# An interleaved rotary embedding: the first megabyte of x in two DMAs of 64 partitions on two queues

## The chip, the cores and the metric

The kernel runs on one core of one Trainium2 chip. The metric is the device time of the program in microseconds, the median of several executions. A profile is one execution more, recorded by the hardware profiler. The engines named below are DVE (VectorE), ACT (ScalarE), POOL (GpSimd) and SP (SyncE); SP and ACT can issue DMAs on hardware queues, POOL issues them on the software queue. All of them are carried out by the core's 16 DMA engines.

## The reference

`x` has the shape (8, 2048, 16, 64): batch, position, head, element, in float32. `cos` and `sin` have the shape (2048, 32). Each pair of neighbouring elements is rotated by the angle of its position:

```python
x_pairs = x.reshape(batch, seq_len, num_heads, head_dim // 2, 2)
x1 = x_pairs[..., 0]
x2 = x_pairs[..., 1]
out1 = x1 * cos - x2 * sin
out2 = x1 * sin + x2 * cos
out = np.stack([out1, out2], axis=-1)
```

The result has the shape of `x` and is float32 again. `x` is 64 MiB and the result is 64 MiB; the tables are 0.25 MiB each.

## The kernel before, in words

The 2048 positions of a batch lie over 128 partitions, 16 neighbouring positions (`K`) in each. A position's 16 heads of 64 elements make a row of 1024 elements, so a batch is a tile of 128 partitions by 16 rows, `xt`, which the kernel keeps in bf16 (4 MiB). There are five such tiles (`NX`), used in turn for the eight batches.

Loads and stores of whole tiles go through POOL's software queue, which converts between float32 in memory and bf16 in the tile (`load`, line 56; `store`, line 59). DVE does the arithmetic in `rotate`: a product with the sine table into `qt` (line 74), a product with the cosine table in place (line 75), and the sum of the two with the neighbours of each pair exchanged (line 80). The sine table holds plus and minus sin alternately, the cosine table each cos twice, both in bf16.

The order of the work is written out by hand (`manual_schedule`); each engine carries out its own list in order.

At the start, SP issues three plain DMAs: the first two rows (`HEAD`) of batch 0 in float32 into a staging tile (`head`, shown as `st`), 8 KiB for each partition and 1 MiB in all (line 84), then `cos` and `sin` (lines 85 and 86). POOL issues five casting loads without waiting: the other 14 rows of batch 0, and batches 1 to 4. ACT converts the staged megabyte to bf16 into the first rows of batch 0's tile (line 91). DVE waits for `sin` and `cos`, makes the tables (lines 93 to 97), and then rotates the first two rows of batch 0, the other 14, and batches 1 to 7.

After each batch POOL issues its store, and from batch 1 on the load of batch b + 4 into the tile that batch b - 1 has left, which waits for that store. After batch 1, POOL first copies one element of the fifth tile (`mark`, line 106), which holds it until that load has landed. Of the last batch 12 rows go out through POOL. The last 4 rows (`TAIL`) are converted to float32 by ACT (line 118) and issued by SP (line 119); ahead of it, a copy of one element on ACT (line 117) waits for the store of the batch before.

The staging tiles and `qt` share one buffer (`tag="work"`), so the first product of DVE also waits for ACT's conversion of the staged megabyte.

Of the kernel before, what the change touches and what calls it, by code (L numbers as in the profile page):

```python
# [2 lines left out]

# [4 lines left out]


@with_exitstack  # L10
def kernel(
    ctx: ExitStack,
    tc: tile.TileContext,
    x: bass.AP,
    cos: bass.AP,
    sin: bass.AP,
    out: bass.AP,
):
    nc = tc.nc
    fp32 = mybir.dt.float32  # L20
    bf16 = mybir.dt.bfloat16
    mult = mybir.AluOpType.mult
    add = mybir.AluOpType.add

    B, S, H, D = x.shape
    P = 128
    K = S // P
    KP = 16
    D2 = D // 2
    HD = H * D  # L30
    NX = 5
    HEAD = 2
    TAIL = 4


    x_t = x.rearrange("b (p k) h d -> b p k (h d)", p=P, k=K)
    out_t = out.rearrange("b (p k) h d -> b p k (h d)", p=P, k=K)
    cos_t = cos.rearrange("(p k) c -> p (k c)", p=P, k=K)
    sin_t = sin.rearrange("(p k) c -> p (k c)", p=P, k=K)

    consts = ctx.enter_context(tc.tile_pool(name="consts", bufs=1))
    xpool = ctx.enter_context(tc.tile_pool(name="xpool", bufs=NX))
    stage = ctx.enter_context(tc.tile_pool(name="stage", bufs=1))

    cos_sb = consts.tile([P, K * D2], fp32)
    sin_sb = consts.tile([P, K * D2], fp32)
    c_tab = consts.tile([P, K, D], bf16)
    s_tab = consts.tile([P, K, D], bf16)

    mark = consts.tile([1, 1], bf16)  # L50
    tiles = {}

    def load(b, k0=0):
        if b not in tiles:
            tiles[b] = xpool.tile([P, K, HD], bf16, name="xt")
        nc.gpsimd.dma_start(out=tiles[b][:, k0:], in_=x_t[b, :, k0:])  # L56

    def store(b, k1=K):
        nc.gpsimd.dma_start(out=out_t[b, :, :k1], in_=tiles[b][:, :k1])  # L59

    def rotate(b, k0, k1):
        nk = k1 - k0
        xp = tiles[b][:, k0:k1]
        qt = stage.tile([P, KP, HD], bf16, name="qt", tag="work")

        def rows(a):
            return a.rearrange("p k (h e) -> p k h e", h=H, e=D)

        def tab(a):
            return dataclasses.replace(  # L70
                a, offset=a.offset + k0 * D, ap=[a.ap[0], [D, nk], [0, H], [1, D]]
            )

        nc.vector.tensor_tensor(out=rows(qt[:, :nk]), in0=rows(xp), in1=tab(s_tab), op=mult)  # L74
        nc.vector.tensor_tensor(out=rows(xp), in0=rows(xp), in1=tab(c_tab), op=mult)  # L75
        q_swap = dataclasses.replace(
            qt, offset=qt.offset + 1, ap=[qt.ap[0], [2, nk * HD // 2], [-1, 2]]
        )
        x3 = xp.rearrange("p k (a j) -> p (k a) j", j=2)
        nc.vector.tensor_tensor(out=x3, in0=x3, in1=q_swap, op=add)  # L80

    with tc.manual_schedule():
        head = stage.tile([P, TAIL, HD], fp32, name="st", tag="work")
        nc.sync.dma_start(out=head[:, :HEAD], in_=x_t[0, :, :HEAD])
        nc.sync.dma_start(out=cos_sb, in_=cos_t)
        nc.sync.dma_start(out=sin_sb, in_=sin_t)
        load(0, HEAD)
        for b in range(1, NX):
            load(b)

        nc.scalar.copy(out=tiles[0][:, :HEAD], in_=head[:, :HEAD])  # L91
        s2 = s_tab.rearrange("p k (i j) -> p (k i) j", j=2)
        nc.vector.tensor_copy(out=s2[:, :, 0], in_=sin_sb)  # L93
        nc.vector.tensor_scalar_mul(s2[:, :, 1], sin_sb, -1.0)  # L94
        nc.vector.tensor_copy(  # L95
            out=c_tab.rearrange("p k (i j) -> p (k i) j", j=2),
            in_=cos_sb.to_broadcast([P, K * D2, 2]),
        )
        for b in range(B):
            if b == 0:  # L100
                rotate(b, 0, HEAD)
                rotate(b, HEAD, KP)
            else:
                rotate(b, 0, KP)
            if b == 1:
                nc.gpsimd.tensor_copy(out=mark, in_=tiles[NX - 1][:1, K - 1, :1])  # L106
            if b < B - 1:
                store(b)

            if b >= 1 and b - 1 + NX < B:  # L110
                load(b - 1 + NX)
        store(B - 1, K - TAIL)

        tail = stage.tile([P, TAIL, HD], fp32, name="st", tag="work")
        nc.scalar.copy(out=tiles[B - 2][:1, 0, :1], in_=tiles[B - 1][:1, K - 1, :1])  # L117
        nc.scalar.copy(out=tail, in_=tiles[B - 1][:, K - TAIL :])  # L118
        nc.sync.dma_start(out=out_t[B - 1, :, K - TAIL :], in_=tail)


# [1 line left out]
_INS = ['x', 'cos', 'sin']  # L123
_OUTS = [((8, 2048, 16, 64), 'float32')]


# [23 lines left out]
```

## Time and profile before

| | |
|---|---|
| median of 3 runs | 317.52 us (317.23 to 317.98) |
| span of the profiled execution | 315.5 us |
| DVE busy | 210.3 us, 67% |
| ACT busy | 6.9 us, 2% |
| POOL busy | 11.7 us, 4% |
| read from and written to memory | 67.63 MB and 67.11 MB |
| first megabyte of x, issue to landing | 4.7 us |
| cos and sin, issue to landing | 13.4 us and 31.7 us |
| tail of 2 MB on SP, issue to landing | 15.5 us |

The profiled execution's own time is its span, from the first instruction to the last; the runs were timed without a profile, and their median is 2.0 us above it. The slices of the page cut the span into 40 equal parts and give each engine's busy share in tenths. A window's line gives its bounds and length, then for DVE, ACT and POOL the busy time with the number of instructions, the granted clock of TensorE (not used here), the busy share of the DMA engines, and GB/s. In short windows a share can be above 1, since a packet counts as a whole where it stands. A line of the waits names who waited, for what, how long in all, how many times, and the longest wait.

### The profile page before, as it was taken

What the parts mean: (1) busy time and instruction counts of PE and PEld (TensorE: products, weight loads), DVE (VectorE), ACT (ScalarE), POOL (GpSimd) and SP (SyncE); (2) the same over time, 40 slices, a digit from 0 to 9 for tenths busy, and PEclk for the clock granted to TensorE, in tenths of its full rate; (3) what the DMA queues carried; (4) which work ended last, traced back from release to release, by engine and by line L of the source; (5) the groups of instructions that cost most, each with busy time, mean ns of one, the idle gap of its engine ahead of it and who ended that gap; (6) DMA issues with size and microseconds to landing.
All of it is one profiled execution on the core that took longest, in us unless ns stands there. A gap on an engine that the chain in (4) does not pass through costs nothing.

```text
span 315.5 us, 125 instructions
## 1 busy us (share of the span) xinstructions
DVE 210.3 (67%) x30; ACT 6.9 (2%) x4; POOL 11.7 (4%) x21
## 2 busy tenths in 40 slices
DVE  0000799999999999999999993899509994000000
ACT  4000000000000000000000000000000000000400
POOL 3000000000000301010000100000000000000000
DMA  9899999999999999999999999999999999999997
GB/s 279 184 261 206 199 220 245 199 199 253 212 199 266 399 449 482 399 332 245 220 399 399 399 199 199 399 532 266 199 241 490 399 399 490 440 399 399 432 432 332
DMA packets 2880, 101.71 MB, mean 322 GB/s; under 512 B 320, under 2 KB 320, under 8 KB 576
## 3 DMA queue, kind: packets, MB, share of 16 engines
q0 software_dynamic: 2304, 98.04, 97.1%
q1 hardware_dynamic: 576, 3.67, 3.0%
HBM read 67.63 MB, written 67.11 MB: 427 GB/s over the span
## 4 chain that ended last, share of the span: by engine, by line
another core or an unknown queue 91%; DMA 1%; ACTq 1%; ACT 1%; issue 0%
DMA st<-in_x_dram 1%; ACTq L145 1%; ACT xt L91 1%; ACT xt L117 0%; ACTq L117 0%
## 5 line engine op out<-in xcount | busy, mean ns | idle before, releaser
L74 DVE TENSOR_TENSOR qt<-xt,s_tab 128x16384 bf16<-128x16384 bf16 (+2 forms) x9 | 69.7, 7743 | 19.1 <-DMA xt<-in_x_dram 18.8
L75 DVE TENSOR_TENSOR xt<-xt,c_tab 128x16384 bf16<-128x16384 bf16 (+2 forms) x9 | 69.7, 7743 | 0.4
L80 DVE TENSOR_TENSOR xt<-xt,qt 128x16384 bf16<-128x16384 bf16 (+2 forms) x9 | 69.7, 7744 | 0.3
L93 DVE CAST s_tab<-sin_sb 128x512 bf16<-128x512 f32 x1 | 0.5, 453 | 33.4 <-DMA sin_sb<-in_sin_dram 33.4
L59 POOL DMA_DIRECT2D out_dram<-xt x8 | 4.3, 534 | 139.9 <-DVE xt L80 139.9
L56 POOL DMA_DIRECT2D xt<-in_x_dram x8 | 4.4, 560 | 72.8 <-DMA out_dram<-xt 72.0
L117 ACT COPY xt<-xt 1x1 bf16<-1x1 bf16 x1 | 0.2, 192 | 288.0 <-DMA out_dram<-xt 288.0
L106 POOL COPY mark<-xt 1x1 bf16<-1x1 bf16 x1 | 2.9, 2929 | 39.6 <-DMA xt<-in_x_dram 39.6
L118 ACT CAST st<-xt 128x4096 f32<-128x4096 bf16 x1 | 3.6, 3598 | 0.0
L91 ACT CAST xt<-st 128x2048 bf16<-128x2048 f32 x1 | 1.9, 1897 | 3.4 <-DMA st<-in_x_dram 3.4
L91 ACT ACT_TABLE_LOAD x1 | 1.3, 1283 | 0.7 <-PEq L134 0.7
L95 DVE CAST c_tab<-cos_sb 128x1024 bf16<-128x1024 f32 x1 | 0.7, 683 | 0.0
L94 DVE TENSOR_SCALAR s_tab<-sin_sb 128x512 bf16<-128x512 f32 x1 | 0.4, 444 | 0.0
L134 POOL MEMSET const-float32-0.0<- 128x1 f32 x1 | 0.1, 100 | 0.2 <-issue 0.2
L134 POOL MEMSET const-bfloat16-1.0<- 128x1 bf16 x1 | 0.1, 102 | 0.0
L134 POOL MEMSET const-float32-1.0<- 128x1 f32 x1 | 0.1, 100 | 0.0
L134 POOL MEMSET const-uint8-127<- 128x1 uint8 x1 | 0.1, 100 | 0.0
## 6 DMA issues: line engine op xcount, KB each, us to landing
xt<-in_x_dram POOLq DMA_DIRECT2D x7, 4096.0 KB, 57.6
out_dram<-xt POOLq DMA_DIRECT2D x1, 6144.0 KB, 47.8
xt<-in_x_dram POOLq DMA_DIRECT2D x1, 3584.0 KB, 22.3
out_dram<-st SPq DMA_DIRECT2D x1, 2048.0 KB, 15.5
st<-in_x_dram SPq DMA_DIRECT2D x1, 1024.0 KB, 4.7
cos_sb<-in_cos_dram SPq DMA_DIRECT2D x1, 256.0 KB, 13.4
sin_sb<-in_sin_dram SPq DMA_DIRECT2D x1, 256.0 KB, 31.7
out_dram<-xt POOLq DMA_DIRECT2D x7, 70.1
```

The lines of the kernel that those rows point to most:

```text
L56: nc.gpsimd.dma_start(out=tiles[b][:, k0:], in_=x_t[b, :, k0:])
L59: nc.gpsimd.dma_start(out=out_t[b, :, :k1], in_=tiles[b][:, :k1])
L74: nc.vector.tensor_tensor(out=rows(qt[:, :nk]), in0=rows(xp), in1=tab(s_tab), op=mult)
L75: nc.vector.tensor_tensor(out=rows(xp), in0=rows(xp), in1=tab(c_tab), op=mult)
L80: nc.vector.tensor_tensor(out=x3, in0=x3, in1=q_swap, op=add)
L91: nc.scalar.copy(out=tiles[0][:, :HEAD], in_=head[:, :HEAD])
L93: nc.vector.tensor_copy(out=s2[:, :, 0], in_=sin_sb)
L94: nc.vector.tensor_scalar_mul(s2[:, :, 1], sin_sb, -1.0)
L95: nc.vector.tensor_copy(out=c_tab.rearrange("p k (i j) -> p (k i) j", j=2), in_=cos_sb.to_broadcast([P, K * D2, 2]),)
L106: nc.gpsimd.tensor_copy(out=mark, in_=tiles[NX - 1][:1, K - 1, :1])
L118: nc.scalar.copy(out=tail, in_=tiles[B - 1][:, K - TAIL :])
L145: with _tile.TileContext(nc) as tc:
```

## The change

The DMA of line 84 becomes two. Each covers 64 neighbouring partitions, with the same two rows of 1024 elements in each, 0.5 MiB. The lower half stays at the head of SP's list; the upper half is issued by ACT, ahead of everything else on ACT's list. All else keeps its order. ACT's conversion now reads what both DMAs have written.

```diff
     with tc.manual_schedule():
         head = stage.tile([P, TAIL, HD], fp32, name="st", tag="work")
-        nc.sync.dma_start(out=head[:, :HEAD], in_=x_t[0, :, :HEAD])
+        nc.sync.dma_start(out=head[: P // 2, :HEAD], in_=x_t[0, : P // 2, :HEAD])
+        nc.scalar.dma_start(out=head[P // 2 :, :HEAD], in_=x_t[0, P // 2 :, :HEAD])
         nc.sync.dma_start(out=cos_sb, in_=cos_t)
         nc.sync.dma_start(out=sin_sb, in_=sin_t)
         load(0, HEAD)
```

## The prediction

> **What bounds the kernel now.** I read the slices of the span first, to see whether any engine or the DMA engines are busy throughout, then the waits, then the order of time, and last the start in steps of half a microsecond.
>
> ```profile
> span 315.5 us, 125 instructions
> DVE 210.3 (67%) x30; ACT 6.9 (2%) x4; POOL 11.7 (4%) x21
> DVE  0000799999999999999999993899509994000000
> DMA  9899999999999999999999999999999999999997
> HBM read 67.63 MB, written 67.11 MB: 427 GB/s over the span
> ```
>
> No slice leaves the DMA engines idle, while DVE does nothing in the first four of the 40 slices and the last six. The kernel moves 67.63 + 67.11 = 134.7 MB, and that is its time. A stretch of pure storing shows the same pace: 417 GB/s from 102 to 141 us, and 428 from 276 to 295.
>
> The waits show that DVE is fed, not feeding:
>
> ```profile
> DVE s_tab L93 <- DMA sin_sb<-in_sin_dram: 33.4, 1, 33.4
> DVE qt L74 <- DMA xt<-in_x_dram: 18.8, 2, 12.4
> ACT xt L91 <- DMA st<-in_x_dram: 3.4, 1, 3.4
> ```
>
> ACT waits 3.4 us for the first megabyte, DVE starts only when sin has landed, and later DVE waits twice for a batch of x. In order of time:
>
> ```profile
> 0.74 1.28 ACT L91 ACT_TABLE_LOAD   x1 [0.74 <-PEq L134]
> 0.74 0.36 SPq L84 DMA_DIRECT2D st<-in_x_dram  x1
> 1.16 0.42 SPq L85 DMA_DIRECT2D cos_sb<-in_cos_dram  x1
> 1.24 2.80 POOL L56 DMA_DIRECT2D xt<-in_x_dram  x5 [0.80 <-PEq L145]
> 1.63 0.42 SPq L86 DMA_DIRECT2D sin_sb<-in_sin_dram  x1
> 5.45 1.90 ACT L91 CAST xt<-st 128x2048 bf16<-128x2048 f32 x1 [3.43 <-DMA st<-in_x_dram]
> ...
> 198.72 8.69 DVE L74 TENSOR_TENSOR qt<-xt,s_tab 128x16384 bf16<-128x16384 bf16 x1 [6.40 <-DMA xt<-in_x_dram]
> ...
> 237.32 8.69 DVE L74 TENSOR_TENSOR qt<-xt,s_tab 128x16384 bf16<-128x16384 bf16 x1 [12.45 <-DMA xt<-in_x_dram]
> ```
>
> The first load of x has all DMA engines to itself until the software queue's casting loads (issued from 1.24 us) come in. The start by windows (the last two columns are the busy share of the DMA engines and the GB/s):
>
> ```profile
> 1.00:1.50 0.50, 0.00 (x0) 0.50 (x1) 0.26 (x1) 1.00 0.00 0
> 1.50:2.00 0.50, 0.00 (x0) 0.50 (x1) 0.50 (x2) 1.00 0.78 131
> 2.00:2.50 0.50, 0.00 (x0) 0.02 (x1) 0.50 (x2) 1.00 0.56 147
> 2.50:3.00 0.50, 0.00 (x0) 0.00 (x0) 0.50 (x2) 1.00 0.91 360
> 3.00:3.50 0.50, 0.00 (x0) 0.00 (x0) 0.50 (x2) 1.00 1.05 442
> 3.50:4.00 0.50, 0.00 (x0) 0.00 (x0) 0.50 (x2) 1.00 0.96 393
> 4.00:4.50 0.50, 0.00 (x0) 0.00 (x0) 0.04 (x1) 1.00 1.01 426
> 4.50:5.00 0.50, 0.00 (x0) 0.00 (x0) 0.00 (x0) 1.00 0.85 324
> ```
>
> Nothing moves before 1.5 us. From 1.5 to 2.5 us 0.5 x (131 + 147) = 139 KB move, from 2.5 to 5.0 us 0.5 x (360 + 442 + 393 + 426 + 324) = 973 KB: the megabyte and the first of cos. After that the casting loads hold the engines. Of the 134.7 MB nothing is added or removed, so a lost microsecond at the start is not absorbed: the DMA engines have no idle time after it. The question is only how well they are used between 1.5 and 5 us.
>
> **The change part by part.** *Issues.* SP keeps three issues of 0.36, 0.42 and 0.42 us, the first for half the bytes. ACT gains one, 0.36 to 0.42 us by those rows. It stands ahead of ACT's table load (1.28 us) and cast; both are covered by ACT's 3.43 us of idle time before the cast, so it costs nothing on the path. Without that cover it would be 0.42 us later for the cast. POOL's queue is untouched. The cast now waits for two transfers. Behind it on ACT stands only the copy at 295.36 us; DVE's first product (L74, 34.66 us) waits for the cast, which ended at 7.35, so 27.3 us of slack cover a late half.
>
> *Completion.* One more transfer brings one more completion and one more semaphore to wait for at the end, where SP's event instructions take 17 to 28 ns: under 0.03 us.
>
> *The way of the two halves.* No row shows a transfer of 64 partitions, so it is bounded from both sides. Lower end: both halves together run as the one transfer did, and two issuers at 0.74 us start the engines sooner. The start-up loss is the time in which 139 KB moved instead of the 389 KB that 973 KB / 2.5 us gives for one microsecond: (389 - 139) / 389 = 0.64 us. Two issuers take at most half of it away, -0.32 us (all of it in the extreme, -0.64). Upper end: each half reaches only half of the destinations, and the two queues, released at the same instant and served in turn, send all engines to the same half at the same time. Then the rate from 2.5 to 5.0 us is half, 195 GB/s, and half of 2.5 us, 1.25 us of engine time, is lost. After 5 us most engines are on the casting loads, whose transfers go over all partitions, and what remains of x goes between them at its former price. If the halves also start one after the other, a second start-up of 0.64 us joins: +1.89 us.
>
> That queues are served in turn is in the rows: cos lands at 1.16 + 13.4 = 14.6 us and sin at 1.63 + 31.7 = 33.3, 18.7 us for 128 rows of 2 KB, eight for each of 16 engines: 2.34 us each, one turn of the software queue. The two halves have equal lists and the same start, so the engines go through them in step; I take the half rate, +1.25 us, less half of the 0.32 us gain at start-up: +1.1 us.
>
> The Trainium skill speaks against the change. "SBUF — State Buffer", section "Door 1: The DMA port swizzle (why [64,N] ≈ [32,N])", says that partitions 0 to 63 reach only eight of 16 ports and puts a 1 MiB transfer at 196 GB/s there against 328 over all partitions; "Can I just issue two DMAs to hit both halves?" says that two concurrent halves gained only 6% over one. Estimated from those figures alone, two halves at 208 GB/s take 5.0 us against 3.2, +1.8 us, so 319.3 us; "DMA: Bandwidth & Descriptors", section "Issuing engines are not separate DMA queues", would alone say that the queue makes no difference. No row here shows either.
>
> *The tables.* At half rate about 139 + 486 = 625 of 1049 KB have moved by 5 us. The rest, 424 KB or 3.2 packets of 8 KB for each engine, stands half on each queue: 1.6 packets ahead of the tables on SP's list. Before, half of cos had passed by 5 us (its landing at 14.6 leaves (14.6 - 5) / 2.34 = about 4 of its 8 turns); now all eight wait, four turns more. Sin is late by (1.6 + 4) x 2.34 = about 13 us, landing near 46; at full rate it stays near 33. DVE starts late by as much. Next in line: store 0, issued at 61.93, goes to 75, but the casting loads run until 102.11 us, when the mark's copy sees the fifth land, so 27 us of slack are left. DVE's later waits take up 6.40 us at the seventh batch and 12.45 at the eighth; only a delay of more than 18.85 us moves the eighth. The cost is nothing; the cover ends at sin later than 52 us.
>
> *Sum.* The profiled span is 315.5 us, so 316.6 us after. The median of the runs, 317.52, lies 2.0 us above the span, for what lies around it; I leave that unchanged: 317.5 + 1.1 = 318.6 us.
>
> **The rivals.** *A: nothing lost.* Halves on two queues could fill both sides of the destinations at once: if engines are out of step by one packet, one is on the lower half while another is on the upper. For it: the same bytes, packets and 16 engines, and start-up spreads the engines (131 and 147 GB/s for a microsecond). Against it: the equal lists. Time: 317.5, from -0.32 to +0.5 us: 317.2 to 318.0.
>
> *B: faster.* Two issuers remove the whole start-up loss, since half the packets have to be made on each queue before the last engine gets its first. Place: 1.5 to 2.5 us; price: -0.64 us, 316.9 us. It decides if over 90% of that loss goes and nothing is lost at 2.5 to 5 us. Against it: 0.74 to 1.5 us is empty anyway, and that wait is not made shorter by a second issuer.
>
> *C: the tables come late enough, or the second queue costs outside the span.* Sin past 52 us would stall the eighth batch, and past that each turn costs 2.34 us; it takes eight turns more instead of 5.6. A third queue might lengthen the 2.0 us around the span. Time 319.6 to 322.
>
> *D: the change does not do what it says.* The head may end no sooner and be cast no sooner; as ACT's cast has 27.3 us of slack, that alone is case A.
>
> **How the numbers follow.** A measurement of this kernel tells about 0.2%, 0.64 us, from no change (three runs lie from 317.23 to 317.98). Forecast: 0.50, its own range 318.2 to 319.5. A: 0.36, B: 0.08, C: 0.06. Slower is the forecast and C, 0.56; same is A, 0.36; faster is B, 0.08. The range goes from 317.2, the lower bound of A, to 319.5, the forecast with a second start-up (317.5 + 1.89, rounded up); outside lie B, C and the edges, under 0.2.
>
> **What would show it.** Right: from 2.5 to 5 us the windows show about 200 to 300 GB/s instead of 389; the cast on ACT starts two to five us later than 5.45; DVE's first cast starts near 46; the waits for x at the seventh and eighth batch shrink by as much in all; the last store's issue on SP (299.08) and the span move by the same 1.1 us. Case A: 389 GB/s stays, cast near 5.4, sin near 33, span 315.5. Wrong at the root: the start unchanged and the end moved, or the start slower and the end not, which would mean that the DMA engines had room later after all.

## The result and the profile after

The changed kernel takes 318.37 us (median of 8 runs, 318.32 to 318.55), the kernel before 317.59 us (8 runs, 317.23 to 317.98). The ratio is 1.0024, 95% interval 1.0015 to 1.0032: slower by 0.24%, 0.78 us. The forecast was 318.6 us, with 317.2 to 319.5 as the range. The profiled execution's span grew by 1.0 us:

```profile
span 316.5 us, 129 instructions
DVE 210.3 (66%) x30; ACT 6.9 (2%) x4; POOL 15.2 (5%) x21
HBM read 67.63 MB, written 67.11 MB: 426 GB/s over the span
```

The last store's issue on SP moved by the same 1.1 us, before and after:

```profile
299.08 0.35 SPq L119 DMA_DIRECT2D out_dram<-st  x1
300.17 0.35 SPq L120 DMA_DIRECT2D out_dram<-st  x1
```

The spans are those of one execution each. A run takes 1.8 us longer than its own span, after the change (318.32 and 316.5 us) as in the kernel before when it was run again (317.42 and 315.6), so nothing was added outside the span. (The 2.0 us of the prediction set the median of the runs against one execution's span.)

The bytes and DVE's work are the same. POOL's 3.5 us more are the one-element copy of the mark (6.4 us long, 2.9 before), which lasted until DVE's current instruction ended in both profiles; the row without the mark below shows that it holds nothing up. The start in order of time (start, length, engine, line):

```profile
0.74 0.55 ACTq L85 DMA_DIRECT2D st<-in_x_dram  x1
0.74 0.55 SPq L84 DMA_DIRECT2D st<-in_x_dram  x1
1.25 2.79 POOL L56 DMA_DIRECT2D xt<-in_x_dram  x5 [0.80 <-PEq L146]
1.35 0.56 SPq L86 DMA_DIRECT2D cos_sb<-in_cos_dram  x1
1.95 0.43 SPq L87 DMA_DIRECT2D sin_sb<-in_sin_dram  x1
5.59 1.28 ACT L92 ACT_TABLE_LOAD   x1 [5.59 <-DMA st<-in_x_dram]
7.89 1.90 ACT L92 CAST xt<-st 128x2048 bf16<-128x2048 f32 x1 [1.01 <-DMA st<-in_x_dram]
37.88 0.45 DVE L94 CAST s_tab<-sin_sb 128x512 bf16<-128x512 f32 x1 [37.88 <-DMA sin_sb<-in_sin_dram]
```

Each half's issue took 0.55 us, where the whole had taken 0.36. The conversion started at 7.89 us instead of 5.45, and DVE at 37.88 instead of 33.38. ACT's table load, which had run at 0.74 us, now came after the lower half, at 5.59 us; the conversion still had to wait 1.01 us for the upper half. The windows of the start (last columns: busy share of the DMA engines, GB/s):

```profile
1.50:2.00 0.50, 0.00 (x0) 0.00 (x0) 0.50 (x2) 1.00 0.00 0
2.00:2.50 0.50, 0.00 (x0) 0.00 (x0) 0.50 (x2) 1.00 0.79 180
2.50:3.00 0.50, 0.00 (x0) 0.00 (x0) 0.50 (x2) 1.00 1.00 344
3.00:3.50 0.50, 0.00 (x0) 0.00 (x0) 0.50 (x2) 1.00 1.20 311
3.50:4.00 0.50, 0.00 (x0) 0.00 (x0) 0.50 (x2) 1.00 1.12 229
4.00:4.50 0.50, 0.00 (x0) 0.00 (x0) 0.04 (x1) 1.00 0.70 148
4.50:5.00 0.50, 0.00 (x0) 0.00 (x0) 0.00 (x0) 1.00 0.90 229
```

Nothing moves until 2.0 us, one window later than before; and then the DMA engines are as busy as before but carry less: 0.5 x (344 + 311 + 229 + 148 + 229) = 631 KB from 2.5 to 5.0 us against 973. The DMA view of two stretches shows which queue was served (queue: packets, MB, share of 16 engines). A packet is one record of this view; for the first megabyte it is 8 KB, one partition's two rows. From 2.0 to 4.0 us:

```profile
DMA packets 68, 0.53 MB, mean 266 GB/s; under 512 B 3, under 2 KB 3, under 8 KB 3
...
q1 hardware_dynamic: 66, 0.52, 99.0%
q10 hardware_dynamic: 2, 0.02, 4.0%
```

and from 4.0 to 6.3 us:

```profile
DMA packets 74, 0.50 MB, mean 217 GB/s; under 512 B 13, under 2 KB 13, under 8 KB 13
...
q10 hardware_dynamic: 60, 0.49, 96.5%
q1 hardware_dynamic: 14, 0.01, 2.6%
```

Queue q1 is SP's, q10 is ACT's. The lower half (0.52 MB) went first, almost alone, then the upper one. In the first stretch 63 packets of 8 KB took 0.990 x 2.0 us x 16 engines, 0.50 us each, and in the second 60 packets took 0.965 x 2.3 us x 16 engines, 0.59 us each. Before the change, from 3.3 to 4.2 us, 45 packets took 0.986 x 0.9 us x 16 engines, 0.32 us each (0.31 us by the median of all packet records):

```profile
q1 hardware_dynamic: 45, 0.37, 98.6%
```

The engines were held, not idle.

By the packet records the first casting packet came at 6.98 us, against 5.11 before. So the first casting load landed 1.87 us later and the next three 2.06 us (mean over the 16 engines; the fourth at 83.56 us against 81.50). But the fifth landed only 1.08 us later, 102.89 against 101.81, and this difference stayed to the end. The DMA view shows where most of these 0.98 us came back. It is cut to 0.6 us in which the last packet of the fifth load starts on each of the 16 engines, so the share times 0.6 us is how long one packet took. Before, from 97.9 to 98.5 us:

```profile
DMA packets 16, 0.52 MB, mean 874 GB/s; under 512 B 0, under 2 KB 0, under 8 KB 0
...
q0 software_dynamic: 16, 0.52, 551.9%
```

and after the change, from 99.8 to 100.4 us:

```profile
q0 software_dynamic: 16, 0.52, 405.3%
```

5.519 x 0.6 = 3.31 us before, 4.053 x 0.6 = 2.43 us after, the length of nearly every other packet of such a load: 0.88 us of the 0.98. These late packets, just ahead of the first store, were not among the steps of the prediction.

### The profile page after: what moved, and what is told of

It reads as the page before. It is cut to its first block, busy times and chain, and to the rows that moved or that the text cites. A ratio compares the mean times of both kernels' runs of the same rounds, so it can differ in the third digit from the quotient of the medians.

```text
span 316.5 us, 129 instructions
## 1 busy us (share of the span) xinstructions
DVE 210.3 (66%) x30; ACT 6.9 (2%) x4; POOL 15.2 (5%) x21
## 4 chain that ended last, share of the span: by engine, by line
another core or an unknown queue 91%; DMA 2%; ACTq 1%; ACT 1%; issue 0%
DMA st<-in_x_dram 2%; ACTq L146 1%; ACT xt L92 1%; ACT xt L118 0%; ACTq L118 0%
## 5 line engine op out<-in xcount | busy, mean ns | idle before, releaser
L107 POOL COPY mark<-xt 1x1 bf16<-1x1 bf16 x1 | 6.4, 6392 | 36.2 <-DMA xt<-in_x_dram 36.2
```

## The experiments

Two questions were open: what makes the start slower (the half of the partitions, or the second queue), and why only half of what the start lost is still lost at the end. Ratios are to the kernel before, run on the same chip in the same rounds.

**The kernel before again** (no edit).

> The kernel before, once more, for its trace. In the two traces at hand the loads after the change land 2.1 us later than before up to the fourth whole tile (83.8 against 81.7 us), and only 1.0 us later from the fifth on (103.1 against 102.1): before, the last packets of the fifth load on all 16 DMA engines took 3.0 to 3.5 us instead of 2.43. Theory S (a stall that belongs to the timing of the kernel before): the same late packets again close to 98 us, the span 315.4 to 316.2 us. Rival (chance): no such packets, the span near 314.5 us, or a stall elsewhere.

317.54 us, ratio 1.0001 (0.9991 to 1.0011). The last packets of the fifth load took 3.2 to 3.6 us at 98 us again; span 315.6 us. The late packets belong to the kernel.

**The changed kernel again** (no edit).

> The changed kernel once more, for its trace. If the gap of the start is a property of the kernel, the fourth load lands near 83.8 us and the fifth near 103.1 again, with no packet of the loads above 2.5 us near 100 us, and the span is 316.5 us within 0.3. If the missing stall was chance, some packets near 100 us take 3 us and the span is near 317.5 us.

318.41 us, ratio 1.0025 (1.0015 to 1.0035), span 316.6 us. The fourth load landed at 83.8, the fifth at 103.15 us (the last of the 16 engines), and no packet of the fifth took over 2.5 us. Both halves of the finding repeat: 2.1 us lost at the start, 1.0 us not lost at 98 us.

**Both halves on SP.**

```diff
-        nc.sync.dma_start(out=head[:, :HEAD], in_=x_t[0, :, :HEAD])
+        nc.sync.dma_start(out=head[: P // 2, :HEAD], in_=x_t[0, : P // 2, :HEAD])
+        nc.sync.dma_start(out=head[P // 2 :, :HEAD], in_=x_t[0, P // 2 :, :HEAD])
```

> The two halves of 64 partitions both on SP, none on ACT: one part of the change alone, without the second queue. Theory H (a half of the partitions is filled at half rate, one half after the other): packets of 8 KB take 0.5 to 0.66 us as after the change, against 0.31 before, the casting loads come in about 2 us later than 5.1 us, and the time is that after the change, 318.4 us within 0.4. Rival Q (the second queue or ACT's issue costs the time): packets of 0.31 us, 317.6 us.

317.55 us, ratio 1.0006 (0.9997 to 1.0015): theory H's time was wrong, though its packets were right for the first half. The start in order of time, and DVE's:

```profile
0.74 0.55 SPq L84 DMA_DIRECT2D st<-in_x_dram  x1
1.24 2.79 POOL L56 DMA_DIRECT2D xt<-in_x_dram  x5 [0.80 <-PEq L146]
1.35 0.57 SPq L85 DMA_DIRECT2D st<-in_x_dram  x1
...
18.18 1.90 ACT L92 CAST xt<-st 128x2048 bf16<-128x2048 f32 x1
...
56.00 0.45 DVE L94 CAST s_tab<-sin_sb 128x512 bf16<-128x512 f32 x1 [56.00 <-DMA sin_sb<-in_sin_dram]
```

The first half moved alone. From 2.0 to 3.7 us its 57 packets took 1.066 x 1.7 us x 16 engines, 0.51 us each:

```profile
q1 hardware_dynamic: 57, 0.47, 106.6%
```

Then the casting loads came in at 3.86 us, ahead of the second half, though that had been issued at 1.35 us. Its packets were taken one after each casting packet, at 0.32 us each. Packets of the whole width took the same 0.32 us there (they did so in the last run below), so between casting packets a half costs no more than the whole would. The fourth load was late by 0.8 us, and the late packets of the fifth took 2.77 us on average instead of 3.31. So in these runs a half costs up to twice the time only where nothing else fills the engines. And sin landing at 56 us cost no time.

**One row each on two queues.**

```diff
-        nc.sync.dma_start(out=head[:, :HEAD], in_=x_t[0, :, :HEAD])
+        nc.sync.dma_start(out=head[:, :1], in_=x_t[0, :, :1])
+        nc.scalar.dma_start(out=head[:, 1:HEAD], in_=x_t[0, :, 1:HEAD])
```

> Two queues as in the change, but each takes one of the two rows of all 128 partitions: the second queue without the halves. Theory H: full rate, some 390 GB/s from 2.5 to 5 us, the casting loads at 5.1 us within 0.5, and the time before, 317.6 us within 0.3. Rival Q: late as after the change, 318.4 us.

317.86 us, ratio 1.0011 (1.0002 to 1.0020). The windows of its start:

```profile
1.50:2.00 0.50, 0.00 (x0) 0.00 (x0) 0.50 (x2) 1.00 0.59 82
2.00:2.50 0.50, 0.00 (x0) 0.00 (x0) 0.50 (x2) 1.00 0.69 123
2.50:3.00 0.50, 0.00 (x0) 0.00 (x0) 0.50 (x2) 1.00 1.02 401
3.00:3.50 0.50, 0.00 (x0) 0.00 (x0) 0.50 (x2) 1.00 1.03 418
3.50:4.00 0.50, 0.00 (x0) 0.00 (x0) 0.50 (x2) 1.00 1.04 393
```

Full rate with two queues: theory H, and Q falls as the cause of the start's 2 us. That leaves 0.4 us. In the trace one DMA engine lies half a microsecond behind the next one, at the fifth load (102.67 us against 102.18) as at the end of the tail (315.26 against 314.75); that this makes the 0.4 us is likely but not shown.

**Every second partition.**

```diff
-        nc.sync.dma_start(out=head[:, :HEAD], in_=x_t[0, :, :HEAD])
+        nc.sync.dma_start(out=head[::2, :HEAD], in_=x_t[0, ::2, :HEAD])
+        nc.scalar.dma_start(out=head[1::2, :HEAD], in_=x_t[0, 1::2, :HEAD])
```

> Two DMAs of 64 partitions on the two queues again, but one takes the even partitions and the other the odd ones, not neighbours. Theory H, in the sharper form that neighbourhood costs (64 neighbouring partitions share half of the ways into the memory on the chip, so a half alone goes at half rate): packets of 8 KB take about 0.31 us, the casting loads come in near 5.1 to 5.5 us, and the third and fourth load land as before (62.4 and 81.7 us within 0.5). Rival N (the number of 64 partitions costs, whichever they are): packets of 0.5 to 0.66 us and the fourth load near 83.8 us.

317.69 us, ratio 1.0004 (0.9995 to 1.0013). The same two queues, the same 64 partitions in each, from 2.0 to 4.0 us:

```profile
DMA packets 90, 0.64 MB, mean 320 GB/s; under 512 B 12, under 2 KB 12, under 8 KB 12
...
q1 hardware_dynamic: 76, 0.52, 83.1%
q10 hardware_dynamic: 14, 0.11, 13.8%
```

After a slow first half microsecond nearly every packet took 0.31 us, on both queues, and the casting loads came at 5.27 us. Neighbourhood is what costs; rival N falls. Neighbouring partitions also read a neighbouring part of `x`, 4 MiB for a half, and no run changes the one without the other, so whether the tile's side or the memory's side costs is not shown. What the number 64 does cost is seen too: the issue took 0.54 and 0.55 us, and the first packet moved at 2.07 us instead of 1.75. The late packets of the fifth load are there (3.48 us), so 64 partitions on two queues do not remove them.

Together the three runs say what the change's 0.8 us needs: rows or every second partition on two queues lost 0.2 to 0.4 us, neighbouring halves on one queue nothing measurable. It takes the halves and the second queue, which puts both of them ahead of the casting loads.

**DVE later.**

```diff
+        spare = consts.tile([P, K * D2], bf16)
+        for _ in range(13):
+            nc.vector.tensor_copy(out=spare, in_=sin_sb)
         s2 = s_tab.rearrange("p k (i j) -> p (k i) j", j=2)
```

> The kernel before with 13 copies of the sine table (about 0.34 us each) ahead of DVE's work, which starts DVE's rotations some 4.4 us later, as in the kernel after the change, and leaves every DMA at the start alone. Theory S with DVE's phase as what sets the stall near 98 us: the stall goes, the fifth load lands near 101 us, and the time falls to about 316.5 us. Rival (the stall is set by something else, or by chance): 317.6 us, as DVE has over 15 us of slack.

317.50 us, ratio 1.0000 (0.9991 to 1.0009). DVE's rotations started 3.4 us later, and the late packets stayed at 98 us, 3.2 to 3.5 us each. DVE's phase does not set them.

**No tables loaded.**

```diff
-        nc.sync.dma_start(out=cos_sb, in_=cos_t)
-        nc.sync.dma_start(out=sin_sb, in_=sin_t)
+        nc.vector.memset(cos_sb, 0.5)
+        nc.vector.memset(sin_sb, 0.5)
```

> The kernel before without the two DMAs of cos and sin; DVE fills both with a constant, so the output isn't the rotation of the reference. All loads move up by the tables' share of the DMA engines, 0.52 MB, about 1.3 us: the fourth load lands near 80.4 us. Five traces (the kernel before twice, both halves on SP, rows on two queues, DVE later) have the first data of the fifth load complete no earlier than 101.25 us, however early they were due. Theory F (nothing of the fifth load completes before 101.25 us, whatever came before): the end stays, 317.5 us. Theory K (the switch from the loads to the first store costs 0.9 us each time): the end moves up by 1.3, to 316.2 us. Theory W (an interval from 100.4 to 101.25 us in which no packet completes, which packets due earlier or later escape): no stall, the end moves up by 2.2, to 315.3 us.

316.25 us, ratio 0.9958 (0.9946 to 0.9971), as theory K had it. The fourth load landed at 80.4 us, and the last packets of the fifth, now starting from 96.7 us on, took 6.053 x 0.6 = 3.63 us:

```profile
q0 software_dynamic: 16, 0.52, 605.3%
```

They move with the loads; no set place in time near 100 us explains them. The casting loads came in at 4.5 us.

**No mark.**

```diff
-            if b == 1:
-                nc.gpsimd.tensor_copy(out=mark, in_=tiles[NX - 1][:1, K - 1, :1])
```

> The kernel before without the copy of one element on POOL that waits for the fifth load, so the second store is issued at about 88 us, not 105, and stands behind the first in the software queue. If the stall near 98 to 101 us belongs to POOL's waiting or to the software queue running short of issued work (only the first store stood behind the fifth load), it goes, and the time falls to 316.5 us. If it is set elsewhere, it stays, 317.5 us.

317.60 us, ratio 1.0007 (0.9998 to 1.0015). The second store was issued at 88.08 us, and the late packets stayed (3.0 to 3.6 us). Neither POOL's waiting nor a short queue makes them.

**The first store ahead of the fifth load.**

```diff
-        for b in range(1, NX):
+        for b in range(1, NX - 1):
             load(b)
...
-            if b == 1:
-                nc.gpsimd.tensor_copy(out=mark, in_=tiles[NX - 1][:1, K - 1, :1])
             if b < B - 1:
                 store(b)
+            if b == 0:
+                load(NX - 1)
```

> The kernel before with the fifth load issued behind the first store (and without the mark), so the software queue goes from the fourth load to the first store near 82 us, and the fifth load follows. Theory K (the first switch from loads to stores costs the late packets): they are the last packets of the fourth load now, near 79 to 82 us, and the time stays 317.5 us. Theory of a set place in time near 100 us: no late packets at 80, and the time is 316.5 to 317.5 us. If the late packets go altogether, 316.5 us.

317.96 us, ratio 1.0004 (0.9996 to 1.0013). The late packets are the last of the fourth load now. They start from 78.5 to 79.4 us and took 3.576 x 1.0 = 3.58 us on average; none stands near 98.

```profile
q0 software_dynamic: 16, 0.52, 357.6%
```

So they stand where the queue first goes over from loads to a store. None of the later such switches shows any.

**More on SP behind the first megabyte**, 0.40 and 0.88 MB (the second with 864 in the place of 392).

```diff
         nc.sync.dma_start(out=head[:, :HEAD], in_=x_t[0, :, :HEAD])
+        nc.sync.dma_start(out=head[:, HEAD:, :392], in_=x_t[0, :, :HEAD, :392])
```

> The kernel before with 0.40 MB more on SP right behind the first megabyte, over all 128 partitions, into a part of the staging tile that nobody reads: at full rate it holds the DMA engines for 0.95 us. The fourth load lands near 82.8 us instead of 81.8. In the traces the last packets of the fifth load lose 0.95 us before the change (1.3 us where the tables were left out and all came 1.4 us earlier) and nothing after it. Theory L (the loss shrinks as the loads come later): hardly anything is left of it, and the time is 317.5 to 317.8 us. Rival P (the loss depends on how the halves left the DMA engines in step with each other): it stays 0.95, and the time is 318.45 us.

> The same with 0.88 MB, 2.1 us, as late as the changed kernel's loads: the fourth load lands near 83.9 us. Theory L: no late packets near 100 us, and the time is that after the change, 318.4 to 318.6 us. Rival P: the late packets stay, 0.95 us, and the time is 319.6 us.

321.43 us, ratio 1.0115 (1.0086 to 1.0144), and 328.71 us, ratio 1.0343 (1.0330 to 1.0356). Both theories missed, since the runs tested something else. In the first of the two:

```profile
st<-in_x_dram SPq DMA_DIRECT2D x1, 392.0 KB, 29.8
cos_sb<-in_cos_dram SPq DMA_DIRECT2D x1, 256.0 KB, 49.4
sin_sb<-in_sin_dram SPq DMA_DIRECT2D x1, 256.0 KB, 68.9
```

The added pieces are two packets for each partition, 16 for each DMA engine, and once the casting loads had come in at 5.07 us each waited out one casting packet. Sin landed at 71.0 us (76.7 in the second), and the first store was issued at 99.6 us (105.3). Now DVE is late, and the time goes with it: in the profiled executions 5.7 us more delay of sin came with 5.7 us more span (321.2 and 326.9). The six runs of the first scatter from 319.99 to 323.01 us, so its median says little. The fifth load had no late packets in either, but the first store was hardly in the queue, or not yet, when it ended, so this says nothing of the changed kernel.

**More over the whole width, on ACT's queue.**

```diff
         nc.sync.dma_start(out=head[:, :HEAD], in_=x_t[0, :, :HEAD])
+        more = head[:, HEAD:].rearrange("p k c -> p (k c)")[:, :1728]
+        nc.scalar.dma_start(out=more, in_=x_t[0].rearrange("p k c -> p (k c)")[:, :1728])
```

> The two runs with more on SP were no test of lateness alone: their packets, two for each partition, pushed the tables back until DVE was late. Here the first megabyte goes over all partitions on SP as before, and 0.88 MB more, one packet for each partition, goes on ACT's queue into a part of the staging tile that nobody reads: 2.1 us at full rate, on both queues, with no half of the partitions. The fourth load lands near 84 us, as after the change, and sin before 45 us. Theory L (the late packets of the fifth load go if the loads come 2 us later): no packet near 100 us above 2.6 us, and 318.5 to 318.8 us. Rival P (they go only where halves of neighbouring partitions left the DMA engines in step): they stay, and 319.4 to 319.8 us.

319.12 us, ratio 1.0048 (1.0034 to 1.0062), between the two theories' times. The fourth load landed at 83.9 us, as late as after the change, the first store was issued at 83.49 us, and the last packets of the fifth, from 99.9 to 100.5 us, took 5.281 x 0.6 = 3.17 us:

```profile
q0 software_dynamic: 16, 0.52, 528.1%
```

So lateness by 2 us does not take the late packets away; theory L falls. Sin landed at 54.9 us, not before 45, and cost nothing visible again.

## Why the prediction was right, and where it was not

The forecast of 318.6 us lies 0.23 us from the result, and the direction was right. The mechanism behind it, about half rate for each half, was right. But that the sum of +1.1 us came out near the measured +0.8 is luck: two errors of about 1 us lie in opposite directions.

**The bound.** Right. The DMA engines are the bound, DVE's later start costs nothing, and the time goes with what the start loses, except at the late packets, below.

**The half rate.** Right in kind: 0.50 and 0.59 us a packet against 0.32. By the windows 391 KB less had moved by 5.0 us, 49 KB of it up to 2.5 us; that is 1.0 us at 389 GB/s, so up to there the sum was right in size too. The row on every second partition shows that it is the neighbourhood. This agrees with the Trainium skill ("SBUF — State Buffer", section "Door 1: The DMA port swizzle (why [64,N] ≈ [32,N])"), which puts each half on eight of 16 ports; no run shows the ports. That page's section "Can I just issue two DMAs to hit both halves?" was right on the halves, and the estimate of +1.8 us from the figures of both sections is closer to the 2.06 us that the start lost than my +1.1. Its sentence that "The only way to hit all 16 ports is one transfer spanning all 128 partitions" does not fit the run with every second partition, if it means that none may be left out: two transfers of 64 partitions each moved at 0.31 us a packet.

**"Served in turn."** The prediction put it that the two queues are "served in turn" and "send all engines to the same half at the same time". The second part holds, the first does not: four packets of SP for each engine went first, then four of ACT. For the rate it came to the same. The second queue mattered all the same: with both halves on SP the casting loads came in between them, and the time was 317.55 us instead of 318.37.

**"After 5 us most engines are on the casting loads."** This failed, and it is the first error. I had taken the 5 us at which the casting loads came in before as a time of theirs. It was not: they came at 3.86 us with both halves on SP, at 4.5 without tables, at 6.98 after the change. By the packet records the engines had carried 73 to 83 KB each of the hardware queues' packets, on average, when the first casting packets came, in 12 of the 14 traces. Without tables it was 65 KB, all there was. With both halves on SP it was 32 KB, the first half, although the second had been issued; what the casting loads wait for is therefore not shown. At a lower rate the same bytes take longer, and so the loss went on to 7 us: 1.87 us later at the first casting packet, and 0.19 us for some two packets of the tables, 0.1 us each, that were then still to come on each engine. That is the 2.06 us.

**The start-up, "two issuers start the engines sooner", -0.16 us in the sum.** Wrong in sign: the first packet moved at 2.10 us instead of 1.75, +0.35 us. In all traces in which the first DMA goes over 64 partitions it moved at 2.07 to 2.10 us, with every second one too; the two-queue run over all partitions started at 1.74. These 0.35 us are part of the 2.06. The issues were priced at 0.36 to 0.42 us and took 0.55.

**"A lost microsecond at the start is not absorbed."** This failed too, and is the second error, of the other sign: 0.98 us of the 2.06 came back between the fourth load and the fifth, 0.88 of it at the last packets of the fifth. The shares near 100% in the slices hid that the engines were held there in the kernel before. A packet's length by the side of its neighbours would have shown it before: 3.31 us against 2.43.

**The tables and their slack.** Sin was expected near 46 us and landed at 37.86; the prediction had 1.6 packets of x and all of the tables still to come when the casting loads came in, but by then all of x and the first packets of cos had gone. The slack was under-sized: the prediction let it end at sin landing at 52 us. It cost nothing visible at 54.9 and 56.0 us, and had run out at 71.0. At 56.0 us, with both halves on SP, DVE no longer waited for x at all, and yet ACT's copy behind the last store but one came at 295.53 us, against 295.36 before: behind the eighth batch there is slack too, which the prediction left out. The waits at the seventh and eighth batch were to shrink by as much as DVE was late. DVE was late by 4.5 us, and they shrank by 3.3, from 18.8 us:

```profile
DVE qt L74 <- DMA xt<-in_x_dram: 15.5, 2, 12.6
```

The rest is the 1.1 us by which the loads came later.

**The rivals.** A (nothing lost) is ruled out by the windows, B (faster) by the first packet and the time, C by sin, which landed at 37.86 us and not past 52, and by the 1.8 us outside the span, which stayed.

**What stays open.** Why the late packets are missing after the change. They stand at the first switch from loads to a store, whatever DVE, the mark or 1.3 to 2 us of earlier or later loads do. Two queues over all partitions keep them, so do halves of every second partition. They are shorter with both neighbouring halves on SP and absent with the halves on two queues. That could come from the order in which the halves leave the DMA engines to each other, but no run changed that order alone, so it is not shown.

Open as well are what the casting loads wait for at the start, and whether the tile's side or the memory's side slows the neighbouring halves.

No version that computes the rotation beat the kernel before.

## What to carry to other kernels

If a transfer has to be split, let each piece still cover the whole spread of partitions: by rows or by every second partition, not by lower and upper half. Neither split was faster than the whole here. A queue's entry time in a profile is not a constant of that queue (here it lay between 3.86 and 7.19 us); ask what it waited for before using it as the end of a loss. Where DMA engines are the bound, compare the length of packets and not only busy shares: a held engine looks like a working one, and a loss or gain can hide in it.

## What the runs showed of the hardware that I had not expected

- As the first DMA on its queue, one over 64 partitions, neighbours or not, took 0.54 or 0.55 us to issue against 0.36 to 0.39 over 128, and its first packet moved at 2.07 to 2.10 us instead of 1.73 to 1.77. Behind another DMA, issues over 128 partitions took 0.42 to 0.58 us too.
- Halves of neighbouring partitions moved 8 KB in 0.50 to 0.59 us on average where nothing else ran, and in 0.32 us between casting packets.
- The software queue's first packets came after 73 to 83 KB for each DMA engine of the hardware queues' work in 12 traces, after 65 KB without tables and after 32 KB with both halves on SP, between 3.86 and 7.19 us.
- The last packets of the load ahead of the first store took 3.2 to 3.6 us on average instead of 2.43 in most kernels, at no later switch, and not at all after the change.
